# Borders between sub-layers ordered step by step for three engines, with squares summed by TensorE

## The chip, the cores and the metric

The kernel runs on one core of a Trainium2 chip. A core has TensorE (matrix products into PSUM; its weight loads are shown as an engine of their own), VectorE (DVE), ScalarE (ACT), GpSimd (POOL) and SyncE (SP), which here issues all the DMAs that load and store. The metric is the device time of one execution in microseconds.

## What is computed

One inference step of a streaming encoder with four layers, for 512 positions of a new stream and 64 of a running one, 576 in all, of width 1024. Each layer has two sub-layers: a token mixer (layers 0 and 3 windowed attention, layer 1 a convolution module, layer 2 a chunked gating MLP) and a ConvFFN (up-projection to 2 x 2816, depthwise convolution over three positions, GELU gate, down-projection). Around each sub-layer stand two RMS norms:

```python
h = _rmsnorm(x, g[0])
...
x = x + _rmsnorm(y, g[1])
h = _rmsnorm(x, g[2])
y, s = _conv_ffn(h, st, p['ffn_w_up'][i], ...)
x = x + _rmsnorm(y, g[3])
```

So between two sub-layers the output y is squared and summed over 1024 channels, scaled, added to x; the new x is squared and summed, and its root scales the next sub-layer's products.

## The kernel before

**Layout.** Channels lie on the 128 partitions, in eight tiles t of 576 positions. The positions are cut in two halves, `HALF`: 256 and 320 (256 of the prompt, 64 of the sample). Matrix products are made of three products each (`mm3`, L228 to 236): a float32 operand is split into a rounded high part and the low part that is left, and high x high, low x high and high x low are added in PSUM. ScalarE makes high parts (weights L203, input `n_hi` L382), another engine subtracts for the low parts (weights L206, input `n_lo` L385). A root's factor is applied when a product leaves PSUM, so products of the next sub-layer can begin with x times its gain before the root is known.

**PSUM.** Products take banks of a pool of six ("mm", `mm_tile`); sums, spreads and transposes take a pool of two ("ms").

**Weights.** `wload` loads a weight by SP into one of two stage buffers, casts it in two halves of 512 columns on ScalarE and subtracts in two halves. `lo_eng` chooses the engine of the subtraction for a sub-layer's first four weights: GpSimd for three of them, VectorE later (`pending`) for the fourth.

**Sums of squares.** `Squares` (L331 to 364) squares each of eight tiles on ScalarE, and GpSimd adds most of them into one accumulator (L352). `RowSums` (L309) then multiplies the accumulator, and the last squares that were kept apart (`OPART`: three, after the convolution two, for the output's second half; one for its first half; none for the input), with a column of ones: two products of one column for the first half, four for the second, per tile. A chain of nine small VectorE steps (`rsqrt_steps`, L281 to 289) makes the reciprocal root, and `spread` (L321, L324) turns it by TensorE into a tile that has it on all partitions.

**The border.** A sub-layer postpones the second half's products of its last output chunks (`left`; eight units of 12 matmuls, after the convolution three of 24). `between` (L519 on) then issues, for seven borders, the postponed units and the first products of the next sub-layer (two "begun" generators, four products for the first half, four to six for the second), with the norms woven in. Early products (`Product.early`, L250 and L251) use high x high and one mixed term per tile as tiles arrive; `late` (L256) adds the rest. The order is written out by the code for VectorE and TensorE, with bounds from the table `PLAN`; ScalarE and GpSimd follow an order that the scheduler plans:

```python
ENGINES = {mybir.EngineType.DVE, mybir.EngineType.PE}
...
with tc.manual_schedule(engines=ENGINES):
    loads = [lambda g=g: next(g) for g in begun for _ in range(2)]
    ...
    for u, products in enumerate(out.late()):
        evacuate = products()
```

Within a unit's turn the evacuation (L438, VectorE adds PSUM to y) comes after a burst of `finish_steps`: scaling y (L459), updating x (L461), high part, square, low part for one tile after another. The attention and the convolution have orders by hand of their own (`AORDER`, `CORDER`); they are not touched.

Of the kernel before, what the change touches and what calls it, by code (L numbers as in the profile page):

```python
# [8 lines left out]
F32 = mybir.dt.float32  # L9
# [8 lines left out]
P = 128  # L18
D = 1024
KD = 8  # L20
# [41 lines left out]

FTAIL = 8
# [27 lines left out]
def encoder_step_kernel(  # L91
# [60 lines left out]
    G.memset(ones, 1.0)  # L152

# [62 lines left out]
    def lo_eng(n, q=0):  # L216
        return V if n >= POOLW else G if n * 2 + q < 4 - DLO else None

# [18 lines left out]

    class Product:


        def __init__(self, ps, items, w=0):
            self.ps, self.items, self.w = ps, items, w

        def all(self):
            mm3(self.ps, self.items)

        def early(self, k):

            l, r = self.items[k]
            T.matmul(self.ps, l[0], r[0], start=(k == 0), stop=False)  # L250
            T.matmul(self.ps, l[self.w], r[1 - self.w], start=False, stop=False)  # L251

        def late(self):

            for k, (l, r) in enumerate(self.items):
                T.matmul(self.ps, l[1 - self.w], r[self.w], start=False, stop=(k == len(self.items) - 1))  # L256

        def step(self, k):
            mm3(self.ps, self.items, k, k + 1)
# [38 lines left out]
    class RowSums:  # L298
# [3 lines left out]
        def __init__(self, name, hf):  # L302
            self.ps, self.hf, self.first = ms_tile(f"{name}_c"), hf, True

        def add(self, parts, last):
            columns = [(0, P, 0, 0), (0, P, 1, P)] + [(0, 64, 2, 256), (64, 64, 2, 192)] * self.hf
            ops = [(t, c) for t in parts for c in columns]
            for q, (t, (o, m, j, a)) in enumerate(ops):
                T.matmul(self.ps[o : o + m, j : j + 1], t[:, a : a + m], ones[:, :1], start=self.first, stop=(last and q >= len(ops) - 1 - self.hf))  # L309
                self.first = False  # L310
# [20 lines left out]
    class Squares:  # L331
# [31 lines left out]
        def sums(self):  # L363
            return (self.rows or RowSums(self.name, self.hf)).all(self.parts)
# [3 lines left out]
    class Norm:  # L368
# [18 lines left out]
        def square(self, t, hf, eng=None):  # L387
            if self.sq[hf] is None:
                self.sq[hf] = Squares(f"{self.name}_{hf}", self.acc, hf, 0)
            self.sq[hf].add(half(x[t], hf), eng)  # L390
# [7 lines left out]
        def spread(self, hf):  # L398
            S.copy(half(self.R, hf), spread(f"{self.name}_{hf}", self.r[hf], hf))
# [16 lines left out]
    order = [(t - q * (q + 1) // 2, q) for t in range(KD + 3) for q in range(3)]  # L416
    order = [a for a in order if 0 <= a[0] < KD]

    class Output:
# [3 lines left out]
        def __init__(self, i, s, bias=None):  # L423
# [4 lines left out]
            self.sq = [Squares(f"{self.name}_{hf}", acc, hf, OPART[1 if s == 3 else 2 if i % 3 == 1 else 0] if hf else APART, u_tile) for hf in range(2)]  # L428
            self.r, self.left = [None, None], []
            self.final = (i, s) == (layers[-1], 3)  # L430
# [4 lines left out]
        def evacuate(self, m, hf, ps, first, last):  # L435
# [7 lines left out]
            if last:  # L443
# [7 lines left out]

        def finish_steps(self, hf, n):

            rb = spread(f"{self.name}_{hf}", self.r[hf], hf)

            def step(t, q):
                ys, xs = half(self.y[t], hf), half(x[t], hf)
                if q == 0:
                    V.tensor_tensor(ys, rb, ys, ALU.mult)  # L459
                elif q == 1:  # L460
                    V.scalar_tensor_tensor(xs, ys, gain(self.i, self.s, t), xs, ALU.mult, ALU.add)  # L461
                    if n is not None:
                        n.high(t, hf)
                        n.square(t, hf)
                elif n is not None:
                    n.low(t, hf)

            return [lambda a=a: step(*a) for a in order]
# [23 lines left out]
        def late(self):  # L492


            sums = {}

            def run(units, a, e):
                for m, items in units:
                    if a == 0:
                        sums[m] = self.psum(m, 1)  # L500
                    mm3(sums[m], items, a, e)
                if e is None:
                    return lambda: [self.evacuate(m, 1, sums[m], self.first, True) for m, _ in units]

            n = len(self.left[0][1])
            if n < KD:
                return [lambda u=u: run([u], 0, None) for u in self.left]
            shared = [lambda k=k: run(self.left, k, k + 1) for k in range(LATEK)]
            return shared + [lambda u=u: run([u], LATEK, None) for u in self.left]

# [8 lines left out]
    def between(out, n, begun):  # L519
# [3 lines left out]
        with tc.manual_schedule(engines=ENGINES):  # L523
            loads = [lambda g=g: next(g) for g in begun for _ in range(2)]
            long = len(out.left[0][1]) == KD
            lead, rate, sum1, spread1, sum0, spread0, last1, ko, lag0, before1, low = PLAN[2 if long else out.s == 3]
            steps = None
            for u, products in enumerate(out.late()):
                evacuate = products()
                if u == long:  # L530
                    chain = out.scale_steps(0)
                if u == lead:
                    steps = out.finish_steps(0, n)
                elif steps and u < len(out.left) - 1 + 2 * long:
                    for step in steps[:rate]:
                        step()
                    steps = steps[rate:]
                if evacuate:
                    evacuate()
                if u == long:  # L540
                    for step in chain:
                        step()
                if u == 0 if long else u % 2:
                    loads.pop(0)()
            for load in loads:
                load()

            parts = [next(g) for g in begun]
            products = [p for part in parts for p in part[0]]
            at = [order.index((k, 2)) + 1 for k in range(KD)]  # L550
            slots = [[(p, k) for p in products[: ko]] for k in range(KD)]
            slots += [[(p, k) for k in range(KD)] for p in products[ko :]]
            slots += [[(p, None)] for p in products]
            chain, done, later, begin = [], len(order) - len(steps), None, len(slots) - len(products)

            def run(upto):
                nonlocal steps, chain, done
                while done < upto:
                    for step in steps[:1] + chain[:1]:
                        step()  # L560
                    steps, chain, done = steps[1:], chain[1:], done + 1

            for q, slot in enumerate(slots + [[]]):
                if q == before1:
                    out.sq[1].begin()
                if q == low:
                    run_all(pending)
                if q == sum1:
                    chain = out.scale_steps(1)
                if q == spread1:  # L570
                    run(len(order))
                    for step in chain:
                        step()
                    chain, later = [], out.finish_steps(1, n)
                if q == max(sum0, begin):
                    rest = n.rms_steps(0)
                for p, k in slot:
                    if k is None:
                        p.late()
                    else:  # L580
                        run(at[k])
                        p.early(k)
            steps, chain = later, rest
            more = [next(g) for g in begun]
            products = [p for part in more for p in part[0]]
            first, others = products[:2], products[2:]
            done = 0

            def upto(q):
                nonlocal done, steps  # L590
                n = min(len(steps), max(0, q - done))
                for step in steps[:n]:
                    step()
                steps = steps[n:]
                done += n

            for k in range(KD):
                while done < at[k]:
                    upto(done + 2)
                    if done > lag0:  # L600
                        for step in chain[:1]:
                            step()
                        chain = chain[1:]
                if k == spread0:
                    for step in chain:
                        step()
# [1225 lines left out]
```

## Time and profile before

| | |
|---|---|
| median of 3 runs | 2876.61 us (2875.34 to 2877.24) |
| profiled execution | 2874.78 us |
| its span | 2873.0 us |
| TensorE busy | 2765.0 us, 96% of the span |
| VectorE busy | 1893.5 us, 66% |
| ScalarE busy | 1133.1 us, 39% |
| GpSimd busy | 548.6 us, 19% |
| mean granted clock of TensorE | 0.976 |

The span runs from the first to the last instruction of one execution; the 1.8 us beyond it lie around the program. Matmuls are pipelined, so a busy TensorE is not one at its peak. The granted clock is 1.00 at 2.4 GHz and 0.50 at 1.2 GHz; a value between is a mean over time.

### The profile page before, as it was taken

The numbers are of one execution on the slowest core, as the hardware profiler recorded it, in microseconds if no ns is written. First come the engines' busy times: TensorE is split into PE (matmuls) and PEld (weight loads), VectorE is DVE, ScalarE is ACT, GpSimd is POOL, SyncE is SP. The second block draws the span as 40 slices with busy tenths as digits, with TensorE's granted clock in tenths as the row PEclk, the third lists the DMA queues.
The fourth block names the chain that finished last, engine by engine and source line by source line (L and its number), as shares of the span: only waits on it lengthen the run. The fifth ranks groups of instructions, "written<-read, shape, count | busy, mean of one in ns | idle before, by whom it ended". The sixth has DMA issues, their size and how long they took to land. (4 is left out here: it accounts for less than half of the span.)

```text
span 2873.0 us, 52726 instructions
## 1 busy us (share of the span) xinstructions
PE 2765.0 (96%) x20665; PEld 2665.2 (93%) x20665; DVE 1893.5 (66%) x4152; ACT 1133.1 (39%) x2371; POOL 548.6 (19%) x1105
## 2 busy tenths in 40 slices
PE   8998999999878999999999998999999998999998
PEld 7888999998666999999999998999999878999998
DVE  5667666657876666667656667666676676766674
ACT  4654433334124443323434224433343574433333
POOL 2134111114000421111402115211113124111111
PEclk9999999999988999999999999999999999999999
DMA  6321322222332222223133221322322421322221
GB/s 167 82 54 52 103 79 84 84 71 70 96 102 54 71 82 89 81 82 93 60 91 99 76 74 47 89 87 76 88 82 71 104 49 46 89 82 81 89 81 57
DMA packets 359182, 230.70 MB, mean 80 GB/s; under 512 B 44595, under 2 KB 349463, under 8 KB 358807
## 3 DMA queue, kind: packets, MB, share of 16 engines
q1 hardware_dynamic: 358934, 227.34, 27.7%
q8 instruction: 163, 2.67, 0.4%
q14 instruction: 85, 0.69, 0.1%
HBM read 212.87 MB, written 7.45 MB: 77 GB/s over the span
## 5 line engine op out<-in xcount | busy, mean ns | idle before, releaser
L235 PE MATMUL f_p<-n_lo,f_w_h 128*128 128x320 f32 (+1 forms) x2688 | 798.7, 297 | 2.4 <-DVE n_lo L385 2.2
L234 PE MATMUL f_p<-n_hi,f_w_h 128*128 128x320 f32 (+1 forms) x2688 | 798.5, 297 | 0.0
L236 PE MATMUL f_p<-n_hi,f_w_l 128*128 128x320 f32 (+1 forms) x2688 | 797.3, 297 | 0.0
L235 PEld LDWEIGHTS f_p<-n_lo,f_w_h 128*128 128x128 f32 x2688 | 510.1, 190 | 5.2 <-DVE n_lo L385 4.8
L234 PEld LDWEIGHTS f_p<-n_hi,f_w_h 128*128 128x128 f32 x2688 | 510.1, 190 | 0.3
L236 PEld LDWEIGHTS f_p<-n_hi,f_w_l 128*128 128x128 f32 x2688 | 510.1, 190 | 0.0
L234 PE MATMUL o_p<-f_ah,f_d_h 128*128 128x256 f32 (+1 forms) x1408 | 418.6, 297 | 1.7 <-ACT f_d_h L203 1.7
L235 PE MATMUL o_p<-f_al,f_d_h 128*128 128x256 f32 (+1 forms) x1408 | 417.7, 297 | 0.0
L236 PE MATMUL o_p<-f_ah,f_d_l 128*128 128x256 f32 (+1 forms) x1408 | 417.2, 297 | 0.0
L203 ACT CAST f_w_h<-f_w_f 128x512 fp32r<-128x512 f32 x352 | 200.4, 618 | 500.3 <-issue 225.4
L438 DVE TENSOR_TENSOR o_y<-o_p,o_y 128x256 f32<-128x256 f32 (+1 forms) x432 | 194.4, 455 | 256.7 <-PE o_p L236 255.8
L745 DVE TENSOR_TENSOR f_ub<-f_p,n_R 128x256 f32<-128x256 f32 x352 | 147.6, 423 | 287.3 <-PE f_p L236 281.4
L234 PEld LDWEIGHTS o_p<-f_ah,f_d_h 128*128 128x128 f32 x1408 | 268.0, 190 | 1.9 <-ACT f_d_h L203 1.9
L235 PEld LDWEIGHTS o_p<-f_al,f_d_h 128*128 128x128 f32 x1408 | 268.0, 190 | 0.2 <-issue 0.2
L236 PEld LDWEIGHTS o_p<-f_ah,f_d_l 128*128 128x128 f32 x1408 | 267.8, 190 | 0.5 <-issue 0.2
L206 DVE TENSOR_TENSOR f_w_l<-f_w_f,f_w_h 128x512 fp32r<-128x512 f32 x328 | 214.1, 690 | 30.7 <-ACT f_w_h L203 26.5
L753 POOL COPY f_fo<-f_ub 128x2 f32<-128x2 f32 x176 | 47.4, 269 | 821.5 <-DVE f_ub L745 812.6
L203 ACT CAST f_d_h<-f_d_f 128x512 fp32r<-128x512 f32 x176 | 101.3, 619 | 227.8 <-PE f_p L235 175.6
L757 DVE SCALAR_TENSOR_TENSOR f_c<-f_ub,f_ct,f_c 128x578 f32<-128x578 f32 x176 | 143.7, 820 | 39.7 <-ACT f_c L756 39.6
L756 ACT ACTIVATE f_c<-f_ub,f_ct 128x578 f32<-128x578 f32 x176 | 151.1, 863 | 7.1 <-DVE f_ub L747 6.7
L766 ACT CAST f_ah<-f_a 128x576 fp32r<-128x576 f32 x88 | 59.3, 674 | 226.0 <-DVE f_a L763 225.6
L758 DVE SCALAR_TENSOR_TENSOR f_c<-f_ub,f_ct,f_c 128x578 f32<-128x578 f32 x176 | 143.3, 816 | 2.8
(361 smaller groups left out, 5907.6 us busy)
## 6 DMA issues: line engine op xcount, KB each, us to landing
f_w_f<-in_ffn_w_up_dram SPq DMA_DIRECT2D x176, 512.0 KB
f_d_f<-in_ffn_w_down_dram SPq DMA_DIRECT2D x80, 512.0 KB
v_w_f<-in_conv_w_pw_dram SPq DMA_DIRECT2D x24, 512.0 KB
v_g<-v_glu SPq DMA_DIRECT2D x128, 77.2 KB
t_wq_f<-in_attn_w_qkv_dram SPq DMA_DIRECT2D x32, 256.0 KB
t_wo_f<-in_attn_w_o_dram SPq DMA_DIRECT2D x32, 256.0 KB
m_wv_f<-in_cmlp_w_in_dram SPq DMA_DIRECT2D x16, 512.0 KB
m_u_w_f<-in_cmlp_w_in_dram SPq DMA_DIRECT2D x16, 512.0 KB
```

The costliest lines, as they stand in the source:

```text
L203: S.copy(hi[:, a:e], st[:, a:e])
L206: eng.tensor_tensor(lo[:, a:e], st[:, a:e], hi[:, a:e].bitcast(F32), ALU.subtract)
L234: T.matmul(ps, lh, rh, start=(i == 0), stop=False)
L235: T.matmul(ps, lh, rl, start=False, stop=False)
L236: T.matmul(ps, ll, rh, start=False, stop=(i == n - 1))
L438: V.tensor_tensor(ys, ps, ys, ALU.add)
L745: V.tensor_tensor(ub[q][:, b : b + 256], ps[q][:, :256], h.R[:, hf * 256 : hf * 256 + 256], ALU.mult)
L753: G.tensor_copy(fo[:, 0, :, c], ub[q][:, 512:514])
L756: S.activation(y, ub[q][:, 2:580], AF.Identity, bias=ct[:, 3, c : c + 1], scale=ct[:, 2, c : c + 1])
L757: V.scalar_tensor_tensor(y, ub[q][:, 1:579], ct[:, 1, c : c + 1], y, ALU.mult, ALU.add)
L758: V.scalar_tensor_tensor(y, ub[q][:, 0:578], ct[:, 0, c : c + 1], y, ALU.mult, ALU.add)
L766: S.copy(a_hi[p], am)
```

## The change

`between` is replaced by an interpreter of a list of steps, one list for each kind of border (output of a mixer, of the convolution or of the FFN; input of an FFN, convolution, MLP or attention). A letter is a step, the digit its tile, unit or product, a further number a count. Capitals mostly belong to the first half, small letters to the second. L is a postponed unit, E its evacuation, Q its square; w loads and casts a weight, l is one half of a weight's low part, on VectorE; D, c, d and I, j, J are sums, root steps and spread of the output's halves; V, X, H, S, N (v, x, h, s, n) scale y, update x, make the high part, square and low part of a tile; G, A, g multiply the squares that wait, F, a, o copy their sums; B, r, R, q and O, k, K, M are the input's root; P, Z are early and late products, U the second half's, e and f their evacuations. The order now holds for ScalarE too.

`BankSums` takes the place of `Squares` for the output's second half (but the last layer's) and for both halves of the input (but the first's): the squares are not added by GpSimd but multiplied with 32 columns of ones, the n-th into column group n mod 4 of one PSUM bank; ScalarE copies the bank, and `RowSums` sums it with a column of 1/32. For the input's first half the bank comes from the six of "mm". `Output`'s first half keeps `Squares`. Weights' low parts of a border are all left to VectorE, and GpSimd's small writes to the edges of `ub` move into the first evacuation. PSUM banks of begun products are taken at their first matmul (`bank`).

```diff
+BORDER = {
...
+    "vf": (
+        "L0 D0 E0 Q0 L1 c0 w0 c08 l02 w1 d0 L2 E1 V0 Q1 V1 X0 X1 H0 l1 H1 l1 S0 S1 V2 w2 V3 X2 N0 E2 N1 H2 P0 P1 X3 P0 Q2 "
...
-LATEK = 2
-OPART = (3, 3, 2)
-DLO = 1
-
-PLAN = [(1, 6, 3, 5, 10, 7, 0, 4, 11, 3, 5), (2, 4, 2, 7, 10, 7, 0, 3, 7, 2, 0), (2, 5, 5, 8, 8, 7, 0, 3, 9, 3, 5)]
+OPART = 3
...
-    def lo_eng(n, q=0):
-        return V if n >= POOLW else G if n * 2 + q < 4 - DLO else None
+    def lo_eng(n):
+        return V if n >= POOLW else None
...
+    class BankSums:
...
+        def add(self, src):
+            q = self.new(f"{self.name}_sq{self.n + len(self.parts)}", [P, 320])[:, : HALF[self.hf][1]]
+            S.activation(q, src, AF.Square)
+            self.parts.append(q)
+
+        def flush(self):
+            if self.ps is None:
+                self.ps = self.tag(f"{self.name}_c")
+            for q in self.parts:
+                g = 32 * (self.n % 4)
+                T.matmul(self.ps[g : g + 32, : HALF[self.hf][1]], ones[:, :32], q, start=(self.n < 4), stop=(self.n >= 4))
+                self.n += 1
+            self.parts = []
+
+        def copy(self):
+            S.copy(self.acc, self.ps[:, : HALF[self.hf][1]])
+
+        def sums(self):
+            rows = RowSums(self.name, self.hf, self.ps)
+            rows.add([self.acc], True, thirty2)
+            return self.ps[:, : 2 + self.hf]
...
-                self.sq[hf] = Squares(f"{self.name}_{hf}", self.acc, hf, 0)
...
+                    self.sq[hf] = BankSums(f"{self.name}_{hf}", self.acc, hf, w_tile, ms_tile if hf else mm_tile)
...
+            def run(m, items):
+                ps = self.psum(m, 1)
+                mm3(ps, items)
+                return lambda **kw: self.evacuate(m, 1, ps, self.first, True, **kw)
...
+        def do(kind, t):
+            hf = int(kind.islower())
+            ys, xs = half(out.y[t], hf), half(x[t], hf)
+            if kind == "L":
+                evacuations[t] = late[t]()
+            elif kind == "E":
+                evacuations[t](square=False)
+            elif kind == "Q":
+                out.sq[1].add(half(out.y[out.left[t][0]], 1))
+            elif kind == "G":
+                out.sq[1].flush()
...
+        with tc.manual_schedule(engines={*ENGINES, mybir.EngineType.Activation}):
+            for step in BORDER[kind].split():
+                for _ in range(int(step[2:] or 1)):
+                    do(step[0], int(step[1]))
...
                 def evacuate(hf=hf, ps=ps):
+                    if hf == 0:
+                        begin()
...
+        out.sq[1].flush()
         yield
         out.block(f"{n}_o", wchunk, 1, kt, True, True, tail=LTAIL, m0=4)
```

The list of the first kind (output of attention or of the MLP, then an FFN) begins:

```python
"L0 L1 E0 Q0 D0 E1 w0 L2 c04 Q1 c04 L3 c0 E2 l0 Q2 l0 d0 w1 E3 L4 V0 Q3 X0 l1 H0 S0 l1 G0 E4 L5 N0 Q4 V1 V2 X1 P0 "
"w2 L6 E5 X2 V3 S1 X3 S2 L7 V4 H1 X4 H2 N1 H3 N2 S3 P0 N3 H4 P1 A0 E6 S4 N4 w3 P0 P1 E7 ..."
```

## Rows read from the trace of the kernel before

**Rows 1.** Waits of TensorE, whole span: us in total, times, longest us.

```profile
PE f_p L250 <- DVE o_y L438: 20.7, 6, 5.6
...
PE o_c L309 <- ACT o_sq L344: 7.1, 3, 2.4
...
PE n_b L321 <- DVE n_o L289: 3.7, 5, 1.1
PE t_kp L235 <- DVE n_lo L385: 2.8, 4, 1.2
...
PE f_p L235 <- DVE n_lo L385: 2.2, 5, 0.6
PE f_p L251 <- DVE n_lo L385: 2.2, 2, 1.9
...
PE m_vp L236 <- DVE n_lo L385: 1.8, 3, 1.0
```

**Rows 2.** Windows over the borders: length; busy PE, PEld, DVE, ACT, POOL; granted clock; DMA share; GB/s.

```profile
202.90:262.30 59.40, 51.34 (x356) 49.56 (x355) 45.13 (x104) 25.42 (x56) 26.58 (x33) 0.91 0.19 54
650.50:705.10 54.60, 50.62 (x358) 48.93 (x357) 43.30 (x105) 26.52 (x58) 27.25 (x27) 0.94 0.14 40
947.40:999.90 52.50, 48.44 (x324) 46.32 (x323) 38.59 (x95) 23.55 (x53) 21.60 (x27) 0.90 0.17 50
1385.30:1445.10 59.80, 55.52 (x405) 54.21 (x404) 47.55 (x112) 28.46 (x65) 26.60 (x25) 0.89 0.23 69
...
2189.80:2245.90 56.10, 52.09 (x381) 50.44 (x380) 41.84 (x101) 24.88 (x56) 26.67 (x25) 0.94 0.20 48
2393.20:2453.20 60.00, 51.86 (x357) 49.93 (x356) 45.25 (x104) 25.53 (x56) 27.37 (x33) 0.91 0.19 54
sum 401.90, PE 361.25 PEld 348.71 DVE 306.64 ACT 179.88 POOL 185.17; mean PE 51.61 PEld 49.82 DVE 43.81 ACT 25.70 POOL 26.45
```

**Rows 3.** Windows inside the border after the first attention, same columns.

```profile
218.60:223.70 5.10, 1.06 (x7) 0.68 (x5) 5.10 (x8) 3.20 (x8) 5.10 (x5) 1.00 0.38 108
223.70:230.50 6.80, 3.77 (x18) 3.80 (x19) 4.88 (x8) 1.97 (x5) 3.13 (x6) 0.50 0.32 92
...
233.90:237.30 3.40, 3.40 (x18) 3.40 (x18) 1.22 (x8) 0.00 (x0) 0.04 (x1) 0.50 0.00 0
```

**Rows 4.** Timeline of that border, all engines: start, us, engine, line, what.

```profile
208.07 2.75 POOL L206 TENSOR_TENSOR f_w_l<-f_w_f,f_w_h 128x512 fp32r<-128x512 f32 x2 [4.58 <-ACT f_w_h L203]
...
209.91 1.19 DVE L461 SCALAR_TENSOR_TENSOR x<-o_y,gains,x 128x256 f32<-128x256 f32 x1
...
211.75 0.47 DVE L461 SCALAR_TENSOR_TENSOR x<-o_y,gains,x 128x256 f32<-128x256 f32 x1
```

**Rows 5.** Groups of VectorE by form: count, busy us, mean ns, idle before.

```profile
L206 DVE TENSOR_TENSOR f_w_l<-f_w_f,f_w_h 128x512 fp32r<-128x512 f32 x328 | 214.1, 690 | 30.7 <-ACT f_w_h L203 26.5 <-PE o_p L236 2.1
...
L385 DVE SCALAR_TENSOR_TENSOR n_lo<-x,gains,n_hi 128x256 fp32r<-128x256 f32 x64 | 55.4, 874 | 0.3 <-ACT n_hi L382 0.3
...
L461 DVE SCALAR_TENSOR_TENSOR x<-o_y,gains,x 128x256 f32<-128x256 f32 x56 | 43.3, 774 | 0.0
```

**Rows 6.** Timeline of TensorE in the convolution.

```profile
724.37 4.29 PE L1343 MATMUL v_pc<-v_g,v_dg 128*32 128x256 f32 x64
728.59 0.39 PE L234 MATMUL v_p<-n_hi,v_w_h 128*128 128x256 f32 x1
728.81 0.28 PE L235 MATMUL v_p<-n_lo,v_w_h 128*128 128x256 f32 x1
```

**Rows 7.** One-column sums of TensorE: the group, and one run of the timeline.

```profile
L309 PE MATMUL o_c<-ones,o_sq 128*128 128x1 f32 (+1 forms) x216 | 26.9, 256 | 7.1 <-ACT o_sq L344 7.1
...
231.26 2.31 PE L309 MATMUL o_c<-ones,o_sq 128*128 128x1 f32 x24
```

**Rows 8.** ScalarE's casts of weights behind a DMA: timeline of a border, waits.

```profile
221.78 1.14 ACT L203 CAST f_w_h<-f_w_f 128x512 fp32r<-128x512 f32 x2 [0.71 <-DMA f_w_f<-in_ffn_w_up_dram]
...
ACT v_w_h L203 <- DMA v_w_f<-in_conv_w_pw_dram: 41.8, 10, 12.0
```

More of the change, by code (lines that the diff above doesn't have):

```diff
@@ L308, in add @@
             for q, (t, (o, m, j, a)) in enumerate(ops):
-                T.matmul(self.ps[o : o + m, j : j + 1], t[:, a : a + m], ones[:, :1], start=self.first, stop=(last and q >= len(ops) - 1 - self.hf))
+                T.matmul(self.ps[o : o + m, j : j + 1], t[:, a : a + m], (ones if weight is None else weight)[:, :1], start=self.first, stop=(last and q >= len(ops) - 1 - self.hf))
                 self.first = False
@@ L450, in scale_steps @@
             return steps
[L452 to L468, printed above, removed]
         def block(self, name, wchunk, per, kt, first, last, tail=4, m0=0):
@@ L492, in late @@
         def late(self):
[L495 to L509, printed above, removed]
+            def run(m, items):
+                ps = self.psum(m, 1)
+                mm3(ps, items)
+                return lambda **kw: self.evacuate(m, 1, ps, self.first, True, **kw)
+            return [lambda u=u: run(*u) for u in self.left]
     CONV_ENGINES = {mybir.EngineType.Activation, mybir.EngineType.DVE, mybir.EngineType.Pool, mybir.EngineType.PE}
@@ L519, in between @@
     def between(out, n, begun):
[L523 to L606, printed above, removed]
-                    chain = []
-                    n.spread(0)
-                    for part in parts:
-                        part[1]()
-                for p in first:
-                    p.step(k)
-            if spread0 >= KD:
-                n.spread(0)
-                for part in parts:
-                    part[1]()
-            chain = n.rms_steps(1) if last1 == 0 else None
-            for q, p in enumerate(others):
-                p.all()
-                if q + 1 == last1:
-                    chain = n.rms_steps(1)
-            if n.keep:
-                n.rest = chain, [part[1] for part in more]
-                return
-            for step in chain:
-                step()
-            n.spread(1)
-            for part in more:
-                part[1]()
@@ new lines, in between, with part, times @@
+        kind = "f" if out.s == 3 else "v" if out.i % 3 == 1 else "x"
+        kind += "f" if n.s == 2 else "avm"[n.i % 3]
+        late, evacuations = out.late(), {}
+        lows, parts, chains, rb = {}, [[], []], {}, {}
+        at = {}
+        def part(hf, j):
+            made = parts[hf]
+            while sum(len(p[0]) for p in made) <= j:
+                made.append(next(begun[len(made)]))
+            return [q for p in made for q in p[0]][j]
+        def times(*key):
+            k = at[key] = at.get(key, -1) + 1
+            return k
```

161 lines of the change are left out of this document (118 added, 43 removed), and 34 rows, old and new, of the table BORDER.

## The prediction

> **What bounds the kernel now.** The page comes first: TensorE is busy for nearly the whole span, every other engine for much less. So another engine can only cost time where TensorE waits for it, and the few slices with a lower TensorE clock tell of a second loss besides idling. The list of TensorE's waits comes next [rows 1]. The reader should see that nearly all of its long rows belong to the seven places where one sub-layer hands over to the next ("borders" from here): 20.7 us for a PSUM bank that VectorE has not yet emptied, 7.1 us for the squares of the output, 3.7 us for a reciprocal root, and 2.8, 2.2, 2.2 and 1.8 us for low parts of the next sub-layer's input. These seven rows add up to 40.5 us. (Part of the 2.8 lies at the kernel's start, outside the borders, and a shorter row not shown lies inside them; I let these cancel.)
>
> The third view cuts out the borders, each from the first postponed output matmul to the last matmul of the next sub-layer's begun products [rows 2]. Three of the seven are of the first kind (59.4 to 60.0 us, granted clock 0.91 each), so the third of them is left out there. The seven take 401.9 us. The missing clock is 0.09 x 59.4 = 5.3, 0.06 x 54.6 = 3.3, 0.10 x 52.5 = 5.3, 0.11 x 59.8 = 6.6, 0.06 x 56.1 = 3.4, and twice 5.4 for the others of the first kind: **34.6 us**. Where it comes from shows inside one border [rows 3]: from 218.6 to 223.7 TensorE worked 1.06 of 5.1 us; the next 6.8 us ran at 0.50, the 1.2 GHz level; after some 3 us at full clock, filled with one-column sums, 3.4 us at 0.50 again. The low stretches follow idling, and in the first kind of border also those sums.
>
> Why VectorE is late is seen beside GpSimd [rows 4]: the same 128x256 update of x took 1.19 us while GpSimd subtracted weights and 0.47 us when it did not. Over all borders the 256-column forms mean 0.774 (x) and 0.874 us (low part) [rows 5].
>
> **The change, part by part.** *GpSimd's work goes.* In a border six low parts of weights (three weights, two halves) move from GpSimd to VectorE: 6 x 0.690 = 4.1 us [rows 5]. The additions of squares for both halves of the input and the second half of the output end. VectorE gets back 8 x (0.774 - 0.47) + 8 x (0.874 - 0.47) = 5.7 us [rows 4, 5]. Its mean load of 306.64/7 = 43.8 us per border [rows 2] becomes about 42. TensorE's busy time of 361.25 us there, less the 34.6 us of clock and plus the 19.4 us worked out below, is 49.5 us per border [rows 2]. So VectorE does not become the bound by its load; only its order matters. I price this part at nothing by itself: TensorE's own work covers it. Without that cover it would cost up to 4.1 us a border.
>
> *Squares by TensorE.* Per border 24 squares are multiplied by a 32-column block of ones, 8 of 256 and 16 of 320 columns. The nearest row is the convolution's product on four column groups: 64 instructions (32 products of 256 or 350 columns, 303 in the mean) from 724.37 to the next matmul at 728.59, so 4.22/32 = 0.132 us each [rows 6], with all groups working side by side. 7 x 24 x 0.132 = **22.2 us added**. They come in six flushes per border, two for each of the three sums (of the second half of the convolution's output, one is issued in that sub-layer). A flush also has an entry and an exit. The matmul behind the run took 0.39 instead of 0.28 us [rows 6]: bounds are 0.11 and 0.39 us per flush, the second if a whole matmul stands alone. I take 0.3, nearer the upper end, since entry and exit both count and groups are not always full: 42 x 0.3 = 12.6 us.
>
> *One-column sums.* For the second half of the output 12 of 16 products go, 8 of 12 at the convolution: 6 x 12 + 8 = 80, of two instructions each. A run of 24 took 2.31 us, 0.096 us each [rows 7]: 160 x 0.096 = **15.4 us saved**. By the busy time over all 216 it would be 26.9/216 = 0.125 each, 20.0 us [rows 7].
>
> The Trainium skill, "TensorEngine Tiling (Array Packing)", section "Performance Considerations" (Instruction Overhead), gives a matmul of one column some 60 cycles, 25 ns at 2.4 GHz; by this the sums saved would be worth 4.0 us, an estimate, and the forecast below would be 11 us later. The rows above show nearly four times that per instruction, and the row decides.
>
> TensorE's net work: 22.2 + 12.6 - 15.4 = **+19.4 us**; bounds 22.2 + 4.6 - 20.0 = +7 and 22.2 + 16.4 - 15.4 = +23.
>
> *The order.* Until now ScalarE was outside the hand order, and a postponed unit's evacuation could stand behind a burst of VectorE steps, after the low parts of many tiles. Now each evacuation is a step of its own, PSUM banks are taken at the first matmul, and ScalarE is in the order too. In the list of the first kind the first early product stands behind six output units on TensorE; the low part that it needs stands on VectorE behind five evacuations, nine root steps, four halves of weights (2.8 us, the largest item) and one tile's scaling and update. So VectorE goes ahead of need by load, and what remains is latency. I keep the 3.7 us of the root and half of the four low-part rows, 4.5 [rows 1], and a low clock of 6.8 us at half speed in two borders, 6.8 us [rows 3]: 15.0 us left over.
>
> *Waits that are added.* A flush waits for ScalarE's squares; behind it on TensorE stand all further matmuls. The first half's input sum takes one of the six "mm" banks, so five serve units and products. And ScalarE now casts the third and fourth weight at a fixed place, waiting there for their DMA; behind the cast stand the high parts and squares, and for those wait VectorE's low parts and then TensorE. The weights' DMAs themselves keep their number; on SP's queue they still wait for a stage buffer, now released by VectorE's two halves instead of GpSimd's. I price this cover at nothing: in the old border the cast at 221.78 waited 0.71 us for its weight [rows 8].
>
> **Sum.** 40.5 + 34.6 - 19.4 - 15.0 = 40.7 us. The profiled execution took 2874.78 us (span 2873.0), so 2834.1; the median of runs, 2876.61, is 1.8 us above it: **2836 us**.
>
> **Rivals.** *A. It goes still better.* Nothing is left over and the net work stays at its lower bound: 40.5 + 34.6 - 7 = 68 us, 2808. For it: VectorE's lead in the list. Against: some latency is always left at a hand-over.
>
> *B. The bank wait survives in part, and with it the clock.* Five banks for units and products, or a late high part, leave 3 us of idling and one low stretch of 6.8 us in each border, as the old borders with a single gap have: 7 x (3 + 3.4) = 45 us left over instead of 15, so 11 us gained, 2866. For it: the old wait reached 5.6 us [rows 1]. Against: evacuations no longer stand behind bursts.
>
> *C. Slower: ScalarE stands at a weight's DMA.* If the third weight lands late, the cast holds up high parts and squares, then low parts, early products and flushes, in every border. Elsewhere in this kernel casts waited 41.8 us in ten places for weights of the convolution, at most 12.0 us [rows 8]. It decides from about 5.5 us of idling per border, which would bring a low stretch of 6.8 us as well: 7 x (5.5 + 3.4) = 62 us left over, against a ceiling of 40.5 + 34.6 - 19.4 = 56: 6 to 7 us slower, 2883. Against it: a border's casts waited only 0.71 us.
>
> *D. The change does not do what it says*: the six flushes run their column groups one after the other. Then the columns cost four times 22.2, 67 us more, and the gain turns into 2903. Against: the convolution's product, where groups of like shape ran side by side [rows 6].
>
> **How the numbers follow.** Chances: forecast 0.55 (2820 to 2850), A 0.15, B 0.19, C 0.06, D 0.02, and 0.03 for a result near the old time. What a measurement of this kernel can tell from no change is about 0.2%, 5.8 us; faster means under 2871. Faster: 0.55 + 0.15 + 0.19 - 0.01 for B's upper edge = 0.88; slower 0.07; the same 0.05. The range reaches from A's 2808 to B's 2866; outside are C, D, the old time and the tails of A and B.
>
> **What would show it.** Right: the L250 row "DVE o_y" and the o_sq row gone from TensorE's waits; granted clock at 0.97 or more in the borders' windows; updates of x and low parts near 0.47 us; squares' runs near 0.13 us each; a first-kind border near 51 us instead of 59.4 (8 of idling and 5.3 of clock less, 2.8 of work and 2 left over more). Wrong: clock still at 0.91 with TensorE fed (then it is the squares or sums that lower it), squares above 0.2 us each, ScalarE's casts behind DMA for several us in the borders, or VectorE idle behind ScalarE while TensorE waits for a low part.

## The result and the profile after

The changed kernel takes **2833.91 us** (median of 4 runs, 2831.09 to 2834.04) against 2875.98 for the kernel before on the same chip: a ratio of 0.9851, 95% interval 0.9838 to 0.9864, or 42 us less. The prediction said 2836, in a range of 2808 to 2866. In the run e1 below, one execution of four took 13310.70 us, in a slow state; it is left out of that run's median (without it e1 stands 21.5 us above after, with it 24.0). The first lines of the page after:

```profile
span 2832.1 us, 52926 instructions
...
PE 2758.0 (97%) x20841; PEld 2637.5 (93%) x20841; DVE 1857.0 (66%) x4194; ACT 1137.5 (40%) x2392; POOL 383.4 (14%) x937
```

GpSimd's busy time fell from 548.6 to 383.4 us; TensorE's share is 97%. The list of TensorE's waits after (us in total, times, longest us) answers to [rows 1]:

```profile
PE v_ro L1413 <- DVE v_glu L1313: 12.8, 2, 8.5
PE v_pc L1389 <- DMA v_g<-v_glu: 11.4, 7, 3.2
...
PE n_c L444 <- ACT n_sq L436: 1.7, 2, 1.0
...
PE f_p L306 <- DVE n_lo L475: 0.7, 1, 0.7
```

The 20.7 us for a bank (o_y) and the 7.1 us for squares of the output (o_sq) are gone. Of the waits inside the borders only the last two rows shown remain, 2.4 us in all. The two costliest rows are the convolution's, to which we come back. The windows over the same seven borders (columns as in [rows 2]):

```profile
202.10:253.00 50.90, 50.90 (x387) 46.29 (x386) 39.04 (x113) 26.36 (x60) 4.07 (x13) 1.00 0.15 43
638.50:692.20 53.70, 52.71 (x402) 47.94 (x400) 37.54 (x104) 28.32 (x65) 2.66 (x5) 1.00 0.18 50
...
sum 358.70, PE 356.34 PEld 324.50 DVE 269.23 ACT 188.45 POOL 18.17; mean PE 50.91 PEld 46.36 DVE 38.46 ACT 26.92 POOL 2.60
```

The reader should see three things. The granted clock is 1.00 in all seven (of the five left out, two are like the first, and the longest took 54.90 us). TensorE is busy for 356.34 of 358.70 us, so 2.4 us of idling are left of 40.65. And the borders last 358.7 instead of 401.9 us: 43.2 us less. The span shrank by 2873.0 - 2832.1 = 40.9, so 2.3 us were given back outside. The stretches between the borders, by the ends of all seven windows of either kernel, show where: five of them, with the kernel's start and end, together became 8.0 us shorter, while the one from the second border to the third, which is the convolution, became longer. Windows over it, first of before, then of after:

```profile
705.10:947.40 242.30, 200.26 (x1557) 166.48 (x1556) 171.63 (x316) 73.22 (x141) 12.33 (x20) 0.90 0.35 90
```

```profile
692.20:944.80 252.60, 206.48 (x1564) 170.20 (x1563) 174.11 (x325) 72.05 (x138) 6.08 (x14) 0.88 0.33 84
```

It grew by **10.3 us**. To see of what, each stretch is split into idling of TensorE, work (its busy time, with stretches at 0.50 counted at half) and what the lower clock took from it while it worked. Time at 0.50 in which TensorE stood idle anyway must count as idling alone. The sums of the windows over all stretches at 0.50 (length, then busy time) give the part at work: over the seven borders of before, then over the convolution before and after:

```profile
sum 68.28, PE 56.28 PEld 55.16 DVE 47.03 ACT 18.92 POOL 27.99; mean PE 5.12 PEld 5.01 DVE 4.28 ACT 1.72 POOL 2.54
```

```profile
sum 47.80, PE 33.41 PEld 25.23 DVE 40.45 ACT 13.22 POOL 0.00; mean PE 4.77 PEld 3.60 DVE 5.78 ACT 1.89 POOL 0.00
```

```profile
sum 61.43, PE 40.62 PEld 32.70 DVE 49.11 ACT 16.48 POOL 0.00; mean PE 5.08 PEld 4.09 DVE 6.14 ACT 2.06 POOL 0.00
```

Half of the busy time in these windows is lost to the clock, so 28.1 us in the borders of before. The same over the whole span gives the last row (us, before to after):

| | idling | lost to the clock at work | work |
|---|---|---|---|
| seven borders | 40.65 to 2.4 | 28.1 to 0 | 333.1 to 356.3 |
| convolution | 42.0 to 46.1 | 16.7 to 20.3 | 183.6 to 186.2 |
| whole span | 108.0 to 74.1 | 50.9 to 24.3 | 2714.1 to 2733.7 |

So the convolution got 4.1 us of idling, 3.6 us of lower clock and 2.6 us of work. Its own list of steps was not edited, but the change puts squares into it. The work is theirs: the one flush of its output's squares (`out.sq[1].flush()` in the diff) came out as four squares, each alone between other products. A timeline of one of them, behind that of a flush of four squares of the same 320 columns in the first border:

```profile
222.63 0.28 PE L306 MATMUL f_p<-n_lo,f_w_h 128*128 128x256 f32 x1
222.84 0.75 PE L444 MATMUL o_c<-o_sq,ones 128*32 128x320 f32 x8
223.52 0.38 PE L305 MATMUL f_p<-n_hi,f_w_h 128*128 128x256 f32 x1
223.74 0.28 PE L306 MATMUL f_p<-n_lo,f_w_h 128*128 128x256 f32 x1
```

```profile
928.68 0.28 PE L278 MATMUL o_p<-v_chi,v_w_h 128*128 128x256 f32 x1
928.89 0.73 PE L444 MATMUL o_c<-o_sq,ones 128*32 128x320 f32 x2
...
929.77 0.28 PE L280 MATMUL o_p<-v_chi,v_w_l 128*128 128x256 f32 x1
```

Without squares these matmuls start 0.12 us apart. From the matmul ahead to the second one behind, less two such steps, four squares cost 223.74 - 222.63 - 0.24 = 0.87 us and the lone square 929.77 - 928.68 - 0.24 = 0.85 us: four together cost hardly more than one. The four lone ones took 3.4 us where one flush would take 0.87.

VectorE's forms answer to [rows 5] (groups by form of after: count, busy us, mean ns):

```profile
L475 DVE SCALAR_TENSOR_TENSOR n_lo<-x,gains,n_hi 128x256 fp32r<-128x256 f32 x64 | 30.1, 493 | 0.7 <-ACT n_hi L472 0.6
...
L638 DVE SCALAR_TENSOR_TENSOR x<-o_y,gains,x 128x256 f32<-128x256 f32 x56 | 25.8, 479 | 0.9
```

The update of x went from 774 to 479 ns and the low part from 874 to 493. The squares on TensorE answer to the forecast from [rows 6] (groups of after, then the flush of the first border with 256 columns):

```profile
L444 PE MATMUL n_c<-n_sq,ones 128*32 128x256 f32 (+1 forms) x224 | 23.1, 417 | 1.7 <-ACT n_sq L436 1.7
...
L444 PE MATMUL o_c<-o_sq,ones 128*32 128x320 f32 x112 | 12.6, 445 | 0.0
```

```profile
219.00 0.28 PE L306 MATMUL f_p<-n_lo,f_w_h 128*128 128x256 f32 x1
219.21 0.64 PE L444 MATMUL n_c<-n_sq,ones 128*32 128x256 f32 x8
219.78 0.38 PE L305 MATMUL f_p<-n_hi,f_w_h 128*128 128x256 f32 x1
220.00 0.28 PE L306 MATMUL f_p<-n_lo,f_w_h 128*128 128x256 f32 x1
```

Read as above, this flush cost 220.00 - 219.00 - 0.24 = 0.76 us, where 4 x 0.132 + 0.3 = 0.83 was forecast for one of the mean width. With 0.87 for 320 columns, the 42 flushes of the forecast would cost 14 x 0.76 + 28 x 0.87 = 35.0 us; forecast 34.8. All squares are busy for 23.1 + 12.6 = 35.7 us.

### The profile page after: what moved, and what is told of

Same layout as the page of the kernel before. It is cut to its first block, busy times and chain, and to the rows that moved or that the text cites. A ratio compares the mean times of both kernels' runs of the same rounds, so it can differ in the third digit from the quotient of the medians.

```text
span 2832.1 us, 52926 instructions
## 1 busy us (share of the span) xinstructions
PE 2758.0 (97%) x20841; PEld 2637.5 (93%) x20841; DVE 1857.0 (66%) x4194; ACT 1137.5 (40%) x2392; POOL 383.4 (14%) x937
## 4 chain that ended last, share of the span: by engine, by line
PE 89%; DVE 4%; DMA 3%; SPq 2%; ACT 1%; issue 1%; POOL 0%; POOLq 0%; ACTq 0%; DVEq 0%
PE f_p L278 13%; PE f_p L279 13%; PE f_p L280 13%; PE o_p L278 9%; PE o_p L280 9%; PE o_p L279 9%; DVE v_cv L1380 2%; PE m_u_p L278 1%; PE m_u_p L280 1%; PE m_u_p L279 1%; PE m_vp L278 1%; PE m_vp L279 1%; PE m_vp L280 1%; PE t_o L1169 1%; PE t_qp L278 1%; PE t_sp L1108 1%
## 5 line engine op out<-in xcount | busy, mean ns | idle before, releaser
L250 DVE TENSOR_TENSOR f_w_l<-f_w_f,f_w_h 128x512 fp32r<-128x512 f32 x352 | 228.9, 688 | 20.3 <-ACT f_w_h L247 18.2
```

Of the source, the lines that this page charges most:

```text
L250: eng.tensor_tensor(lo[:, a:e], st[:, a:e], hi[:, a:e].bitcast(F32), ALU.subtract)
```

## The experiments

All times are medians; ratios are to the kernel before on the same chip. The runs are on several chips, and the ratios' intervals are some 2 us wide to either side or more, so a difference of 2 us between two runs tells nothing. Edits are to the kernel after, but for the last.

**e1, squares back to GpSimd.** The new order and `BankSums` replaced by `Squares` (GpSimd adds, one-column sums).

```diff
+        def flush(self):
+            pass
...
-                    self.sq[hf] = BankSums(f"{self.name}_{hf}", self.acc, hf, w_tile, ms_tile if hf else mm_tile)
+                self.sq[hf] = Squares(f"{self.name}_{hf}", self.acc, hf, 0)
...
```

> The new order stays, but the squares of the borders are added by GpSimd again and summed by one-column products (flushes and copies of banks fall away). Theory (GpSimd's work slows VectorE and comes late, so TensorE's summing buys more than it costs): TensorE's work falls by about 17 us (44 us of sums and squares to 27), but VectorE loses some 4 us a border again and the last additions are late, so 2 us of idling a border and low clock in three of them return, 14 + 10 us: about 2841 us, granted clock 0.98. Rival (the order alone brought the gain, the squares on TensorE are pure cost): 17 us faster than the changed kernel, 2817 us, no low clock in the borders.

Measured: 2855.38 us (three executions, 2852.79 to 2860.49; 0.9924, 0.9904 to 0.9943), 21.5 above after. The direction is the theory's, the size some three times its own. The profiled execution is the slowest of the three. The first border and the sum over the seven (windows of e1):

```profile
201.90:258.90 57.00, 54.03 (x363) 51.59 (x362) 45.58 (x113) 25.58 (x57) 22.18 (x31) 0.91 0.15 43
...
sum 392.30, PE 369.54 PEld 355.00 DVE 311.41 ACT 180.88 POOL 135.40; mean PE 52.79 PEld 50.71 DVE 44.49 ACT 25.84 POOL 19.34
```

In the first border idling is 3.0 us (57.00 - 54.03) instead of the 8.1 of before, yet the clock is 0.91 again, just as in [rows 2]. Over the borders idling rises to 392.30 - 369.54 = 22.8 us, 20 more than after for the theory's 14, and the low stretches come back in all seven borders, some 29 us at work for the theory's 10. TensorE now waits 5.4 us in all for GpSimd's sums (n_acc), and for low parts in several borders. Its work falls by about 16 us, for 17 expected: the theory had the work right, and idling and clock, the clock above all, too small.

**e2, low parts back to GpSimd.** Three of the border's weights in four get their low parts there.

```diff
-    def lo_eng(n):
-        return V if n >= POOLW else None
+    def lo_eng(n, q=0):
+        return V if n >= POOLW else G if n * 2 + q < 3 else None
```

> The new order stays, but three of a border's four first weights have their low parts made by GpSimd again, at the place where the weight is loaded. Theory (GpSimd's presence slows VectorE's updates and low parts, and GpSimd frees the stage buffers later): the forms of 256 columns rise from about 0.47 to 0.7 us, 1 to 3 us of waits a border: 2841 to 2855 us. Rival (the order has enough slack, where the low parts are made doesn't matter): within 3 us of the changed kernel.

Measured: 2842.07 us (0.9885, 0.9870 to 0.9899), 8.2 above after; the theory holds at its lower edge. The update of x takes 652 ns in the mean, for about 0.7 us expected. The clock stays at 1.00 in six borders of seven; TensorE now waits three times for low parts of the input, 3.1 us in all, and once 2.4 us for the output's root.

**e9, the order alone.** Both edits together: squares and low parts on GpSimd as before the change, under the new lists of steps.

> The new hand order with GpSimd's work kept: squares added by GpSimd and three low parts of the border's weights on GpSimd. If the two prices measured one at a time (24.0 us for the squares, 8.2 us for the low parts) add up: 2833.9 + 32.2 = 2866, so the order alone is worth 10 us. Theory: they add up or more, since the additions of squares stand behind the subtractions on GpSimd's queue: 2864 to 2885. Rival: they overlap, since both show as the same late sums and low clock, and one late sum hides the other: 2857 to 2862, the order alone worth 14 to 19 us.

Measured: 2870.57 us (0.9983, 0.9973 to 0.9992). The theory holds: the two prices more than add up (21.5 + 8.2 = 29.7, or the 32.2 of the text above, against 36.7 measured). **The order alone is worth 0.17%, some 5 us** (2 to 8 by the interval). Its windows, waits and VectorE's forms say why:

```profile
202.10:259.30 57.20, 53.43 (x362) 51.68 (x361) 45.54 (x107) 25.41 (x57) 28.53 (x37) 0.91 0.14 40
...
sum 404.80, PE 373.66 PEld 359.32 DVE 316.70 ACT 181.00 POOL 187.20; mean PE 53.38 PEld 51.33 DVE 45.24 ACT 25.86 POOL 26.74
```

```profile
PE f_p L306 <- DVE n_lo L480: 6.9, 4, 2.0
PE o_c L376 <- DVE o_o L344: 6.1, 7, 2.4
```

```profile
L641 DVE SCALAR_TENSOR_TENSOR x<-o_y,gains,x 128x256 f32<-128x256 f32 x56 | 41.5, 758 | 0.9
```

The bank wait is gone, but low parts and the output's root take its place; idling is 404.80 - 373.66 = 31.1 us (40.65 before), the clock in the first border 0.91 as before, and the update of x takes 758 ns beside GpSimd (774 before). With e1 and e2 this makes a table of two by two under the new order:

| | squares on GpSimd | squares on TensorE |
|---|---|---|
| low parts on GpSimd | 2870.57 (e9) | 2842.07 (e2) |
| low parts on VectorE | 2855.38 (e1) | 2833.91 (after) |

The squares are worth 28.5 or 21.5 us, the low parts 15.2 or 8.2. The lists were written for VectorE without GpSimd beside it; whether lists written for GpSimd's timing would be worth more than 5 us was not tried.

**e3, one group.** The squares multiplied by all 128 columns of ones.

```diff
-                g = 32 * (self.n % 4)
-                T.matmul(self.ps[g : g + 32, : HALF[self.hf][1]], ones[:, :32], q, start=(self.n < 4), stop=(self.n >= 4))
+                T.matmul(self.ps[:, : HALF[self.hf][1]], ones, q, start=(self.n == 0), stop=(self.n == 7))
```

> Each square is multiplied with all 128 columns of ones instead of 32 columns in one of four groups; same sums, other weight of the last product. Theory (four groups work side by side; 24 products of a border take 4.4 us): alone each takes 4 passes, 0.43 us for 256 and 0.53 us for 320 columns, 11.9 us a border, so 7 x 7.5 = 53 us slower than the changed kernel, 2886 us. Rival (the 4.4 us are mostly the switching to and from column groups): under 20 us slower.

Measured: 2872.69 us (0.9988, 0.9979 to 0.9998), 38.8 above after. A group of e3 (count, busy us, mean ns):

```profile
L443 PE MATMUL o_c<-o_sq,ones 128*128 128x320 f32 x112 | 32.9, 432 | 0.0
```

Where four groups had 12.6 us of busy time for the output's 112 instructions, one has 32.9. The groups do work side by side, rival D falls, and without them nearly the whole gain would be gone. The cost is 38.8/168 = 0.23 us per square, below what the theory took; the clock stayed at 1.00 in the borders, so squares in this form do not lower it.

**e4, late evacuations.** In the three borders of the first kind, evacuations five to seven, with their squares and the flush of these, are put behind the steps of the next tiles.

```diff
-"w2 L6 E5 X2 ... A0 E6 S4 N4 w3 P0 P1 E7 P0 P1 V5 ... H7 l3 P2 F0 ..."
+"w2 L6 X2 ... A0 S4 N4 w3 P0 P1 P0 P1 V5 ... H7 l3 E5 Q5 E6 Q6 E7 Q7 G0 P2 F0 ..."
```

> Only the list of the three borders of the first kind: the evacuations and squares of the last three output units move behind the low parts and updates of the first half. Theory (the old wait was for a PSUM bank behind a burst of VectorE steps, and idling of some us brings a low clock): TensorE waits 3 to 5 us at the first early product of the third weight's product in each of the three, and a stretch at 0.50 follows: 3 x (4 + 3.4) = 22 us slower, 2856 us. Rival (low clock came from the one-column sums, not from idling): at most 12 us slower and the clock in those borders stays at 1.00.

Measured: 2843.29 us (0.9886, 0.9871 to 0.9901), 9.4 above after. One wait and one low stretch per border appear (waits, timeline, window of e4):

```profile
PE f_p L305 <- DVE o_y L528: 7.5, 3, 2.5
```

```profile
224.76 0.38 PE L305 MATMUL f_p<-n_hi,f_w_h 128*128 128x256 f32 x1 [2.49 <-DVE o_y L528]
```

```profile
226.40:229.80 3.40, 3.40 (x25) 2.09 (x23) 0.49 (x2) 0.00 (x0) 0.00 (x0) 0.51 0.69 198
```

So a late evacuation does cost by the bank wait and by the clock behind it: 2.5 us of idling and 1.7 of clock (half of 3.4 us). That is 4.2 us per border, against 9.4/3 = 3.1 in the median; the other stretches must have run some 3 us faster than in after, and why was not followed. The theory's mechanism is shown, at under half its size; the rival's number was nearer, its claim of an untouched clock was not.

**e5, ScalarE's order back to the scheduler** (the list rules VectorE and TensorE alone).

```diff
-        with tc.manual_schedule(engines={*ENGINES, mybir.EngineType.Activation}):
+        with tc.manual_schedule(engines=ENGINES):
```

> The lists stay, but ScalarE's instructions in the borders follow the scheduler's plan again; VectorE and TensorE keep the lists. Theory (the plan puts casts of weights and squares in another order; the list holds the high parts early): VectorE waits for high parts, TensorE for low parts, 1 to 2 us a border, 2840 to 2848 us. Rival (ScalarE has so little to do, 25 of 50 us a border, that its order doesn't matter): within 3 us of the changed kernel.

Measured: 2834.07 us (0.9857, 0.9844 to 0.9871), the same as after, as the rival expected. The third engine in the title brings nothing by itself.

**e6, e10, e7: the convolution's ten microseconds.** The convolution's own list begins, on VectorE, with the root of the border's last sum (R), then low parts (l2), which free the stage buffers for the next weights. Timelines of before and after around that point (DVE and SPq rows picked):

```profile
698.02 0.16 DVE L281 TENSOR_SCALAR n_v<-n_c 128x3 f32<-128x3 f32 x1 [0.20 <-PE n_c L309]
...
704.24 0.38 SPq L224 DMA_DIRECT2D v_w_f<-in_conv_w_pw_dram  x1
...
710.42 21.23 SPq L1312 DMA_DIRECT2D v_g<-v_glu  x32
```

```profile
691.44 0.16 DVE L336 TENSOR_SCALAR n_v<-n_c 128x3 f32<-128x3 f32 x1 [5.40 <-PE n_c L364]
...
695.08 2.45 SPq L268 DMA_DIRECT2D v_w_f<-in_conv_w_pw_dram  x2
701.57 21.02 SPq L1358 DMA_DIRECT2D v_g<-v_glu  x32
```

Before, the root began at 698.02, 7.1 us ahead of the border's end at 705.1; after, at 691.44, 0.8 us ahead of 692.2, with VectorE idle for 5.40 us in front of it. The border ends 12.9 us earlier, but the weights' DMA starts only 9.2 and the copies of v_g only 8.9 us earlier: some 4 us late against TensorE, as much as the idling added. e6 moves the last sum five steps of products (U) ahead in the border's list; e10 puts two low parts ahead of the root in the convolution's list; e7 does both.

```diff
-        "U3 n5 s6 U0 v7 h6 U2 x7 U0 U3 n6 h7 U2 s7 U0 n7 U3 U0 U3 U1 g0 U1 o0 U2 U1 O0 U2 U1"
+        "U3 n5 s6 U0 v7 h6 U2 x7 U0 U3 n6 s7 U2 h7 g0 U0 n7 o0 U3 U0 O0 U3 U1 U1 U2 U1 U2 U1"
...
-    "R0 h2 R08 y0 h2 R1 l2 R2 l2 t0 h3 ..."
+    "h2 l22 h2 R0 R08 y0 R1 R2 t0 h3 ..."
```

> One list, the border into the convolution: the last square, flush, copy and sum of the second half of the input come about five products earlier. Theory (the convolution starts with VectorE's root steps, which wait for that sum; its first weights' low parts, and so the weights' DMAs, stand behind them, and the convolution takes some 10 us more than before since TensorE now arrives there earlier than they do): root steps, first weights' DMA and everything behind come 2 to 3 us earlier, 2831 to 2832 us. Rival (the convolution is paced by something of its own): no difference, within 1 us.

> As the run with the early sum, and the convolution's list begins with its first weight's low parts ahead of the root steps. Theory: the first weights' DMA is issued about 3 us earlier again, and the convolution's chain of copies and weights behind it, 2828 to 2830 us. Rival (the chain hangs on the gated tiles, not on the weights): the root comes 1.2 us later and nothing is gained, 2832 to 2835 us.

> After with only the convolution's first steps changed (two halves of a weight's low part ahead of the root's steps). Theory: the low parts free the stage buffers, so the third and fourth weight start earlier and the stage before the last border but five shortens as far as in the run with both edits: 1.5 to 3 us gained, 2831 to 2832.5. Rival: as long as the sum of the half comes late, VectorE's root steps and not the buffers end the wait, and delaying them behind low parts costs what it gains: 2833.5 to 2836.

Measured: e6 2829.29 us (0.9842, 0.9828 to 0.9855), e7 2827.39 (0.9834, 0.9821 to 0.9848), e10 2826.68 (0.9830, 0.9813 to 0.9846). The weights' DMA and the window over the convolution, of e6, then of e10:

```profile
692.55 3.38 SPq L268 DMA_DIRECT2D v_w_f<-in_conv_w_pw_dram  x2
```

```profile
691.90:940.20 248.30, 205.52 (x1565) 169.05 (x1564) 172.19 (x318) 72.09 (x138) 6.06 (x14) 0.89 0.33 86
```

```profile
689.83 7.49 SPq L268 DMA_DIRECT2D v_w_f<-in_conv_w_pw_dram  x2
```

```profile
692.20:937.90 245.70, 202.77 (x1564) 166.14 (x1563) 172.77 (x323) 72.21 (x138) 6.66 (x14) 0.91 0.33 85
```

The earlier the weights' DMA starts against the border's end (after 2.9 us behind it, e6 0.7 behind, e10 2.4 ahead), the shorter the convolution: 252.6, 248.3, 245.7 us. That is the theory's mechanism. Each gained more than its theory: by medians 4.6 us (e6), 6.5 (e7) and 7.2 (e10). By the ratios, each to the kernel before on its own chip, it is 2.6, 4.9 and 6.0, and the intervals overlap with after's, e6's above all; the windows, 4.3 and 6.9 us shorter in e6 and e10, show the gain apart from this. e10 alone gained against its rival, and e6's edit on top of it (e7) added nothing: both edits shorten the same chain, and whichever frees the buffers first takes the gain. All three beat the kernel before; e10 and e7 can't be told apart. What is left in e10 against before (245.7 for 242.3) is not waiting: its idling is 245.70 - 202.77 = 42.9 us, for 42.0 before, and 16.1 us are lost to the clock at work, for 16.7. It is work, of which the four lone squares are the most.

**e8, low parts to VectorE in the kernel before.** `DLO` tells how many of the first four weights' low parts VectorE makes.

```diff
-DLO = 1
+DLO = 4
```

> The kernel before with one number changed: the low parts of all four first weights of a border go to VectorE, at the place where the fourth's went, so GpSimd keeps only the additions of squares. Theory (GpSimd's presence was half of VectorE's lateness, the old order the other half): VectorE gains some 3 us and pays 4.1 us a border, in one burst ahead of late products: between 10 us faster and 10 us slower than before, 2866 to 2886 us, the bank wait in three borders shrinks from 5.6 us to 2 to 4. Rival (the subtraction on GpSimd was the main cause): 30 us faster, bank waits under 1 us, clock 0.98.

Measured: 2922.34 us (1.0162, 1.0148 to 1.0176), 47 slower. Both theories missed. Waits of TensorE, then a timeline of the first border of e8 (DVE, SPq, ACT and PE rows):

```profile
PE f_p L250 <- ACT f_w_h L203: 47.1, 7, 10.8
```

```profile
222.70 2.48 DVE L206 TENSOR_TENSOR f_w_l<-f_w_f,f_w_h 128x512 fp32r<-128x512 f32 x4
...
224.04 8.77 SPq L224 DMA_DIRECT2D f_w_f<-in_ffn_w_up_dram  x4
...
228.03 1.14 ACT L203 CAST f_w_h<-f_w_f 128x512 fp32r<-128x512 f32 x2 [4.70 <-DMA f_w_f<-in_ffn_w_up_dram]
...
228.70 0.58 PE L250 MATMUL f_p<-n_hi,f_w_h 128*128 128x256 f32 x1 [10.77 <-ACT f_w_h L203]
```

The old order makes all pending low parts in one burst, at 222.70, after all the tiles. Only then are the two stage buffers free, SP issues the next weights at 224.04, ScalarE's cast waits 4.70 us for them, and TensorE 10.77 us for the cast. The new lists spread the low parts (l) among the tiles; that is what makes this part of the change affordable.

## Why the prediction was right, and where it was not

The total was right to 2 us. The net work of its sum held; three of its errors (the clock counted too high, the rest left over too high, the convolution missing) cancelled, and that is luck.

**Ceiling.** Waits of 40.5 and clock of 34.6 us were named as the two losses, and both went: idling in the borders from 40.65 to 2.4, the low clock to nothing. But 34.6 is too large as a loss. It takes the whole of every stretch at 0.50, and [rows 3] shows that in the one of 6.8 us TensorE was busy for 3.77: the rest is idling, which the 40.5 holds already. At work the clock took 28.1 us, so the ceiling was 6.5 too high (6.0 counted twice, the rest rounding).

**Net work of TensorE, +19.4.** Over the whole span work rose from 2714.1 to 2733.7 us, so by 19.6. In the borders it rose by 23.2, in the convolution by 2.6, and outside both it fell by 6.2: the windows of after also hold matmuls that stood outside them before (that is most of the 8.0 us by which the other stretches shrank). The price of a flush held (35.0 for 34.8), but for the convolution's, which came as four lone squares. Split into columns (0.132) and flush (0.3) it did not: a lone square costs 0.85 and four of them 0.87, so nearly all of it comes with the first square. The Trainium skill, "TensorEngine Tiling (Array Packing)", section "Key Properties", states that a change of tiling mode drains TensorE and gives it no price; by the timelines above the whole flush of four squares, columns and drains together, takes 0.76 to 0.87 us. What the sums that went had cost is not measured apart. (The prediction's 49.5 us per border for TensorE should read 49.4; nothing hangs on it.)

**Left over, 15.0 us.** This is the first term that failed: 2.4 us and no clock were left, so it was 12.6 too large. The root's wait, half of the low parts' and two low stretches were to stay. Inside the borders 0.7 us for a low part stayed, and 1.7 us for squares came instead; two waits for roots, 1.1 and 0.8 us, lie just behind the windows.

**What lies behind a border.** The second failed step is one that the prediction did not contain: it asked what covers the moved work inside the border, but not what the old border's tail had covered for the next stage. The convolution's chain (sum, root, low parts, stage buffers, DMA, copies) had 7.1 us of cover and kept 0.8. That cost 4.1 us of idling and 3.6 of clock; the lone squares' work of 2.6 us makes it 10.3. In spans: 38.3 of idling and 28.1 of clock gone in the borders, less 19.6 of work and less 7.7 lost in the convolution, plus 1.8 won elsewhere, are the 40.9.

**Which part of the change brings it.** The prediction named the order as what recovers the waits and priced GpSimd's removal "at nothing by itself". e9, e1 and e2 show this to be wrong: the order alone is worth 5 us. With GpSimd at work the forms of VectorE stay slow, sums come late and the clock stays at 0.91. Under the order, the squares on TensorE are worth 21 to 29 us and the low parts 8 to 15. Without the order the low parts cost 47 (e8), and with squares on one column group little would be left (e3). The parts need each other; the forecast had the total right without knowing which part earns it.

**Added waits.** ScalarE's fixed casts cost nothing (e5). In the borders no wait for a cast's DMA reaches TensorE; rival C did not happen in the new order, while e8 shows its mechanism in the old one. Rival B's bank wait did not survive; e4 shows what it would have cost. A's 2808 was not reached; without the convolution's loss the result would have been 2833.9 - 10.3 = 2824, some 16 us short of it, mostly the net work (19.6 for A's 7).

**Signs.** As the prediction listed them: the two wait rows gone, clock over 0.97, updates and low parts near 0.47 (0.479 and 0.493), squares 0.14 to 0.17 each from their start to that of the next matmul (0.19 to 0.22 with the gap ahead and the slower matmul behind), first border 50.9 for "near 51". This last was met by other terms than those listed: 8.1 of idling and 3.6 of clock at work less, 3.2 of work more, nothing left over.

## What to carry to other kernels

When a stage gets shorter, look at what its tail was covering: a chain over several engines behind it (here a sum, a root, the release of buffers, a DMA) must be moved forward as well, or part of the gain is given back in a stage that nobody edited. Count idling at a low clock once, as idling. Issue squares four at a time: here a lone one cost as much as four. An engine off the critical path can be worth removing for what it does to a neighbour's durations, and a hand order earns little until those durations let it. Test the parts of such a change together and apart, since their prices do not add.

## What the runs showed of the hardware

**VectorE beside GpSimd.** The same 128x256 update of x, mean over a run: 774 ns before and 758 in e9 with both of GpSimd's jobs, 652 with the low parts alone (e2), 581 with the squares alone (e1), 479 with neither. The Trainium skill, "SBUF — State Buffer", section "Who interferes with whom", states that VectorE's operations with two inputs in SBUF contend with GpSimd's reads; the runs agree, and show the price here: 774/479, some 60% longer in the mean.

**The clock also falls behind one-column sums, with no wait.** e1's first border idles 3.0 us and e9's 3.8 where before idled 8.1, and all three were granted 0.91; e2's idles 1.0 at 1.00. What e1, e9 and before share, and e2 and after don't, are the squares added by GpSimd, with 52 instead of 28 one-column sums in a border (after the convolution 44 in before). e9's first border shows them apart from a wait. A timeline and two windows of e9:

```profile
227.99 0.72 PE L364 MATMUL o_c<-ones,o_acc 128*128 128x1 f32 x8
228.64 2.31 PE L364 MATMUL o_c<-ones,o_sq 128*128 128x1 f32 x24
230.88 0.61 PE L364 MATMUL n_c<-ones,n_acc 128*128 128x1 f32 x4
```

```profile
227.90:231.90 4.00, 4.00 (x43) 3.88 (x42) 2.12 (x7) 0.00 (x0) 2.49 (x9) 1.00 0.45 131
231.90:235.30 3.40, 3.40 (x18) 3.40 (x17) 2.06 (x14) 0.00 (x0) 0.00 (x0) 0.50 0.00 0
```

The list of TensorE's waits from 221.5 to 235.3 is empty, and it was busy for 4.00 of the 4.00 us in which these sums stand; behind the 36 in a row the clock fell all the same. In before the second low stretch of [rows 3], at 233.9, stands right behind such a run too ([rows 7]), with the last wait 7 us earlier. In after at most 12 such sums stand in a row, and the clock stays. But a wait is enough as well: in e4 TensorE stood still for 2.49 us, worked on at full clock for 1.6 us, and ran the next 3.4 us at the lower level. So part of what the squares on TensorE are worth seems to be clock that the sums they replace had cost; how large a part is not shown, since no run changes the number of sums alone.
